# Prompt logits as two products over stacked parts, and five gate units between the mixer's projections and its gated linear unit

## The chip, the cores and the metric

The kernel runs on one core of one Trainium2 chip. The metric is the device time of one execution in microseconds (us), median over runs. Some work of the core goes on side by side: TensorE (PE, matrix products; PEld is its weight load), VectorE (DVE), ScalarE (ACT), GpSimd (POOL), and the DMA queues, most of which are issued by SyncE (SP). Each engine works through its own instructions in a fixed order and waits where an operand or a buffer isn't ready.

## What is computed

One decoder layer for 1024 prompt tokens and 64 sample tokens (8 sequences of 8), model width 1024. The change touches the token mixer between two feed-forward halves:

```python
q, k, v, xs, ga, gb = split(u @ w_in)                 # 512, 512, 512, 512, 1024, 1024 columns
z = q·k * 64**-0.5 + bias                             # 8 heads of 64; key before query only
log_beta = log_sigmoid(z)
log_keep = where(mask, log_beta - z, 0)
after = reverse_cumsum(log_keep) - log_keep
a = where(mask, exp(log_beta + after), 0) @ v         # stick-breaking attention
b = GLU(gelu(S5_scan(xs)))                            # diagonal state-space scan, 32 groups
h = h + g2 * ((sigmoid(ga) * (a @ w_branch_a) + sigmoid(gb) * (b @ w_branch_b)) @ w_out)
```

## The kernel before

Every float32 matrix is held as two float16 parts, hi and lo, and a product is three products: hi·hi, hi·lo, lo·hi. All 1088 token columns (with padding 1092) go through TensorE as three chunks of 364.

The mixer has this order in the code. First the projection of `xs` (the scan's input), then k, then q, each as units of 128 output rows (`project`, L226: 3 chunks of 24 matmuls, so 72 per unit), then v with tokens on the partitions (L1344: 18 chunks of 24 matmuls). The scan `ssm_run` runs for four groups m = 0 to 3, and its steps are issued between these units (list `steps`). Each group sends its result to HBM in eight transfers (`yd`, L995) and loads its matrices in eight and one (`m`, L976 and `ca`, L978) before its last block of matmuls (L988, L990). Then comes the gated linear unit `glu`: its input is split into parts on ACT and DVE (tile `z2`), its products are L226 with operand `z2`, and its output `ob` goes to HBM (`od`, L1444).

Then comes the prompt attention, by pairs of heads (p = 0 to 3), each with 12 steps of 128 keys against the queries not before them: two runs of 128, 256, 384 and 512 queries, and four more of 512. A step computes the logits of two heads (L1087), `ae` and `az` from them (L1094 on ACT, L1095 on DVE), exp, ln and parts (`weights_of`, L1012 to L1028, over both heads at once), sums over keys by triangular products (L1024, L1100), and the product with v (L1105). The sample tokens' attention is issued between. L1056 on ACT, in `scaled_pair`, writes the hi part of q and k back in place, once per pair and operand.

The 16 units of `ga` and `gb` (gate units) have no reader until the branches. One is issued in `glu`, 15 with the attention, paced by a count of its steps. Each evicts three chunks on ACT (L1357) and stores them to HBM (`gd`); the branches read them back. After the attention, `o2` is split and branch b's first products (L216) run.

The code gives the work its dependences and a preference; a scheduler in the compiler puts each engine's instructions in one static order, by its own estimate of times.

The logits of a pair before are three products per head, each over 64 partitions:

Of the kernel before, what the change touches and what calls it, by code (L numbers as in the profile page):

```python
# [9 lines left out]
F32 = mybir.dt.float32  # L10
F16 = mybir.dt.float16
# [9 lines left out]
P = 128  # L21
# [5 lines left out]
NP = 1024  # L27
# [78 lines left out]
class Weights:  # L106
# [88 lines left out]
    def next(self):  # L195
        self.ahead()
        return self.ready.pop(0)
# [835 lines left out]

def halves_of(t, p):

    return t.bitcast(F16).rearrange("p a (t two) -> p a two t", two=2)[:, p, :, :NP]


def scaled_pair(k, qT, kT, p):


    nc = k.nc
    v = nc.vector
    scratch = k.small.tile([P, 16], F32, tag="sq", bufs=1)
    m, r, sc, b = (scratch[:, i:j] for i, j in ((0, 2), (2, 4), (4, 8), (8, 9)))
    for i, t in enumerate((qT, kT)):
        absmax(k, t[:, p, :NP], m[:, i:i + 1])
    nc.gpsimd.partition_all_reduce(r, m, P, ABSMAX)
    v.tensor_single_scalar(sc[:, 2:4].bitcast(I32), r.bitcast(I32), 0x7F800000, op=ALU.bitwise_and)
    v.tensor_scalar(sc[:, 2:4], sc[:, 2:4], 2.0 ** -20, 2.0 ** -14, op0=ALU.max, op1=ALU.mult)  # L1050
    v.reciprocal(sc[:, 0:2], sc[:, 2:4])
    for i, t in enumerate((qT, kT)):
        hi, lo = (halves_of(t, p)[:, j] for j in range(2))
        h = k.part_slot()
        split(k, h, lo, t[:, p, :NP], sc[:, i:i + 1])
        nc.scalar.activation(hi, h, AF.Copy)  # L1056
    cs = k.cs_qk[:, p]
    v.tensor_mul(cs[:, 0:1], sc[:, 2:3], sc[:, 3:4])
    v.tensor_mul(b, r[:, 0:1], r[:, 1:2])
    v.scalar_tensor_tensor(b, b, float(DH), k.bias_m, op0=ALU.mult, op1=ALU.add)  # L1060
    s, inv = pow2_scale(k, b)
    v.tensor_single_scalar(cs[:, 1:2], s, 1.0, op=ALU.min)
    v.tensor_scalar(cs[:, 2:3], inv, 1.0, -1.0, op0=ALU.max, op1=ALU.mult)
    return cs[:, 0:1], (cs[:, 1:2], cs[:, 2:3])


def attend_prompt(k, qT, kT, vt, pairs, scales):

    nc = k.nc
    for p in pairs:  # L1070
        (qh, ql), (kh, kl) = ([halves_of(t, p)[:, j] for j in range(2)] for t in (qT, kT))
        inv, c = scales[p]
        for qc in range(2):
# [3 lines left out]
            for j in range(top, -1, -1):  # L1077
# [4 lines left out]
                def logits(az, ae):  # L1082
                    pz = [k.psz.tile([P, 512], F32, tag="z") for _ in range(2)]
                    for i, (a, b) in enumerate(((kh, qh), (kh, ql), (kl, qh))):
                        for h, ps in enumerate(pz):
                            r = slice(64 * h, 64 * h + 64)
                            nc.tensor.matmul(ps[:, :n], a[r, P * j:P * j + P], b[r, cols], start=i == 0, stop=True,  # L1087
                                             skip_group_check=True)
                    for h, ps in enumerate(pz):
                        b = k.bias[:, 2 * p + h:2 * p + h + 1]  # L1090
                        if j >= 4 * qc:
                            nc.tensor.matmul(ps[:, :P], k.ident16, k.causal, start=False, stop=True,
                                             skip_group_check=True)
                        nc.scalar.activation(ae[:, h, :n], ps[:, :n], AF.Abs, scale=inv, bias=b)  # L1094
                        nc.vector.tensor_scalar(az[:, h, :n], ps[:, :n], inv, b, op0=ALU.mult, op1=ALU.add)  # L1095

# [10 lines left out]
                if (qc, j) == (1, 3) and p < 3:  # L1107
                    scales.append(scaled_pair(k, qT, kT, p + 1))
                if j:
# [165 lines left out]
def mixer_a(k, dr, out, u, ivu, par, ds, gd, od):  # L1275
# [50 lines left out]
    def run(n, sink):  # L1326
        for g in range(n):
            for q in range(2):
                project(g, q, sink)
                for m in steps.pop(0) if steps else ():  # L1330
                    next(ssm[m])

    run(2, keep(kT))
    nc.sync.dma_start(out["kT"].rearrange("m p t -> p m t"), kT)
    run(2, keep(qT, DH ** -0.5))
    for g in range(2):
        w = k.w.next()
# [15 lines left out]

    def to_gate(m, iv):
        def f(c, ps):
            t = k.gate_slot()
            nc.scalar.activation(t, ps, AF.Copy, scale=iv)  # L1357
            (nc.gpsimd if m == 15 else nc.sync).dma_start(gd[m, :, c * CH:(c + 1) * CH], t)
        return f

    gates = [lambda g=g, q=q: project(g, q, to_gate, g == 7) for g in range(8) for q in range(2)]
    k.gate_slot = lambda: k.ring.tile([P, T], F32, tag="r", name="gate")[:, :CH]

    def between():
        gates.pop(0)()

    k.cs_qk = k.co.tile([P, 4, 3], F32, tag="csqk")
    k.part_slot = lambda: k.ring.tile([P, NP], F16, tag="hs", bufs=1)
    scales = [scaled_pair(k, qT, kT, 0)]
    ivb = glu(k, dr, ds, od, between)  # L1370
# [137 lines left out]
def trunk_kernel(ctx, tc, dr, out):  # L1508
# [12 lines left out]
    f2 = ffn_order(dr["ffn2_w_in"], [dr["ffn2_w_out_" + c] for c in "abc"])  # L1521
    order = f1 + [(dr["w_in"][i], KD, 256) for i in (6, 7, 2, 3, 0, 1, 4, 5)]
    order += [(dr["glu_w"][i], 4, 256) for i in range(2)]
    order += [(dr["w_in"][i], KD, 256) for i in range(8, 16)]
    order += [(dr["w_branch_" + n][g], 4, 512) for n in "ba" for g in range(2)]
# [293 lines left out]
```

## Time and profile before

| what | value |
|---|---|
| median of 3 runs (lowest, highest) | 2405.1 us (2403.59, 2409.14) |
| profiled execution, its time | 2406.67 us |
| its span, first to last instruction | 2405.0 us |
| mean granted TensorE clock, of full | 0.982 |

The span is a single execution's; some 1.7 us of its time lie around it. The profiled execution is 1.6 us above the median, so a sum made in its span is moved to the median as a difference.

### The profile page before, as it was taken

How to read it: one execution, taken by the hardware profiler on the slowest of the kernel's cores; microseconds unless marked ns; L12 is line 12 of the kernel's file. 1: busy time of each engine (PE TensorE's matmuls, PEld its weight loads, DVE VectorE, ACT ScalarE, POOL GpSimd, SP SyncE). 2: the span in 40 equal slices, each digit the busy share in tenths (PEclk: the TensorE clock that was granted, in tenths of full speed). 3: DMA queues.
4: the chain of work that ended last, by engine and by line, in shares of the span. 5: the costliest groups of instructions: out<-in, count | busy, mean ns of one | idle time of the engine just before them, and what ended most of it. 6: DMA issues, size and time to landing. Idle time of an engine off the chain costs nothing.

```text
span 2405.0 us, 43066 instructions
## 1 busy us (share of the span) xinstructions
PE 2322.1 (97%) x18535; PEld 1630.6 (68%) x18535; DVE 1689.3 (70%) x3042; ACT 953.8 (40%) x1193; POOL 143.1 (6%) x193
## 2 busy tenths in 40 slices
PE   5999999999999999999999998999999999999997
PEld 2677778777787566775444444656688878888884
DVE  4776688876897726457889887597487654777735
ACT  3443331233331522155778776324343331333403
POOL 0000000000000000001233200000000000000000
PEclk8999999999999999799999999999999999999999
DMA  8133334433343144444233314522101133111302
GB/s 309 53 110 110 110 112 137 151 127 123 119 154 111 66 145 136 113 138 153 73 110 107 106 37 174 173 80 86 61 36 53 52 127 120 64 54 54 128 19 75
DMA packets 90351, 256.54 MB, mean 107 GB/s; under 512 B 12384, under 2 KB 49632, under 8 KB 79920
## 3 DMA queue, kind: packets, MB, share of 16 engines
q1 hardware_dynamic: 84400, 236.16, 28.4%
q0 software_dynamic: 5312, 17.34, 2.4%
q8 instruction: 145, 2.38, 0.4%
q14 instruction: 46, 0.38, 0.1%
q10 hardware_dynamic: 448, 0.29, 0.0%
HBM read 204.10 MB, written 49.66 MB: 106 GB/s over the span
## 4 chain that ended last, share of the span: by engine, by line
PE 44%; DVE 6%; ACT 3%; DMA 2%; issue 1%; POOL 0%; DVEq 0%; POOLq 0%; ACTq 0%
PE u L477 14%; PE u L242 10%; PE u L226 9%; PE u L216 3%; PE z L1087 2%; PE o L1105 1%; PE P L1024 1%; PE P L1100 1%; DVE wl L102 1%; DVE mx L89 1%; PE z L1148 1%; DMA wf<-in_w_in 1%; ACT x L392 0%; DVE mh L102 0%; DMA wf<-in_ffn_w_out_a 0%
## 5 line engine op out<-in xcount | busy, mean ns | idle before, releaser
L226 PE MATMUL u<-u,wh 128*128 128x364 f16 (+1 forms) x1632 | 393.0, 319 | 9.5 <-ACT u L394 6.3
L242 PE MATMUL u<-h,wh 128*128 128x272 f16 (+1 forms) x2304 | 365.9, 280 | 6.1 <-DVE h L102 6.0
L101 ACT ACTIVATE wh<-wf,sc 128x1024 f16<-128x1024 f32 (+2 forms) x128 | 182.3, 1427 | 377.1 <-PE u L242 145.0
L242 PEld LDWEIGHTS <-wh 128*128 128x128 f16 x2816 | 273.1, 97 | 67.1 <-issue 10.4
L89 DVE TENSOR_REDUCE mx<-wf 128x1 f32<-128x1024 f32 (+2 forms) x134 | 210.9, 1597 | 138.7 <-DMA wf<-in_ffn_w_in 77.6
L477 PE MATMUL u<-u,wh 128*128 128x272 f16 x1728 | 272.9, 279 | 0.3 <-DVE q L499 0.3
L477 PEld LDWEIGHTS <-wh 128*128 128x128 f16 x2304 | 221.7, 98 | 63.6 <-issue 19.6
L226 PE MATMUL u<-u,wl 128*128 128x364 f16 (+1 forms) x816 | 260.2, 319 | 1.1 <-DVE wl L102 1.1
L226 PEld LDWEIGHTS <-wh 128*128 128x128 f16 x1824 | 176.6, 98 | 122.2 <-issue 26.0
L102 DVE SCALAR_TENSOR_TENSOR wl<-wf,sc,wh 128x1024 f16<-128x1024 f32 (+2 forms) x128 | 208.7, 1631 | 64.2 <-ACT wh L101 63.4
L242 PE MATMUL u<-h,wl 128*128 128x274 f16 (+1 forms) x1152 | 227.6, 279 | 0.0
L477 PEld LDWEIGHTS <-w3h 128*128 128x128 f16 x1728 | 167.1, 97 | 38.9 <-issue 4.5
L477 PE MATMUL u<-fac,w3h 128*128 128x272 f16 (+1 forms) x1152 | 182.5, 279 | 0.0
L477 PE MATMUL u<-u,wl 128*128 128x272 f16 x864 | 170.3, 278 | 0.0
L82 POOL PARTITION_ALL_REDUCE am<-mx x106 | 54.7, 521 | 1906.9 <-DVE mx L89 1827.7
L242 PEld LDWEIGHTS <-wl 128*128 128x128 f16 x1408 | 136.6, 97 | 29.4
L226 PEld LDWEIGHTS <-wl 128*128 128x128 f16 x912 | 89.4, 98 | 69.0 <-issue 17.9
L477 PEld LDWEIGHTS <-wl 128*128 128x128 f16 x1152 | 111.9, 97 | 24.7 <-issue 0.4
L226 PEld LDWEIGHTS <-aside 128*128 128x128 f16 x864 | 83.0, 97 | 50.5 <-issue 1.7
L477 PE MATMUL u<-fac,w3l 128*128 128x272 f16 x576 | 113.8, 279 | 0.0
L503 ACT ACTIVATE h<-h,iv 128x546 f32<-128x546 f32 x36 | 27.0, 749 | 206.2 <-DVE h L502 206.2
L477 PE MATMUL u<-fac,wh 128*128 128x272 f16 x576 | 92.8, 284 | 3.8 <-DVE st L519 3.8
(430 smaller groups left out, 3922.8 us busy)
## 6 DMA issues: line engine op xcount, KB each, us to landing
wf<-in_ffn_w_in SPq DMA_DIRECT2D x44, 1024.0 KB, 4.8
aw<-in_ada_w SPq DMA_DIRECT2D x72, 512.0 KB, 4.7
wf<-in_w_in SPq DMA_DIRECT2D x16, 1024.0 KB, 5.1
wf<-in_ffn_w_out_a SPq DMA_DIRECT2D x16, 640.0 KB, 3.9
xd<-xr SPq DMA_DIRECT2D x16, 546.0 KB, 2.8
x<-xd SPq DMA_DIRECT2D x16, 546.0 KB, 7.1
xd<-x SPq DMA_DIRECT2D x6, 1456.0 KB, 6.5
sg<-gd SPq DMA_DIRECT2D x16, 546.0 KB, 4.2
```

Source lines behind the costliest of these rows:

```text
L82: k.nc.gpsimd.partition_all_reduce(r, m, P, ABSMAX)
L89: k.nc.vector.tensor_reduce(m, src, axis=axis, op=ALU.max, apply_absolute_value=True)
L101: r = k.nc.scalar.activation(hi, src, AF.Copy, scale=s)
L102: k.nc.vector.scalar_tensor_tensor(lo, src, s, hi, op0=ALU.mult, op1=ALU.subtract)
L216: k.nc.tensor.matmul(ps[:, c, :n], wt[:, cols], act(kt, part)[:, c * CH:c * CH + n], start=kt == 0 and j == 0, stop=kt == nk - 1 and j == 2)
L226: k.nc.tensor.matmul(ps[:, :n], wt[:, cols], act(kt, part)[:, c * CH:c * CH + n], start=kt == 0 and j == 0, stop=kt == nk - 1 and j == 2)
L242: k.nc.tensor.matmul(ps[:, a:b], wt[:, cols], act(kt, part)[:, a0 + a:a0 + b], start=kt == 0 and j == 0, stop=kt == nk - 1 and j == 2)
L477: nc.tensor.matmul(t[:, c0:c1], wt[:, kt * P:kt * P + P], act(kt, part)[:, c0 - 240:c1 - 240], start=first and kt == 0 and j == 0, stop=kt ...
L503: nc.scalar.activation(h2, h2, AF.Silu, scale=iv)
L1024: nc.tensor.matmul(acc[:rk, h, :], k.tri[:rk, :rk], part[:, h, :], start=first and j == 0, stop=True, skip_group_check=True)
L1087: nc.tensor.matmul(ps[:, :n], a[r, P * j:P * j + P], b[r, cols], start=i == 0, stop=True, skip_group_check=True)
L1100: nc.tensor.matmul(acc[:, h, q0:], k.earlier, part[:, h, :], start=False, stop=True, skip_group_check=True)
```

## The change

Two things change. The parts of q and k are stacked on partitions, so that a head's logits are two products over 128 partitions: kh stands on 64 of them and kl on the other 64, against qh on both halves in the first product and ql on both in the second (kl·ql, which was left out before, comes along). The stacking is done by 12 transfers per pair inside SBUF (L1058, 64 rows by 1024 columns of float16 each, 128 KB), from slots that `ah` of the attention uses too. `az` of the second head of each pair is computed on ACT (L1096) and no longer on DVE. The copies L1056 are gone.

Of the gate units, two are issued between q and v, two between v and `glu`, one in `glu` and 11 with the attention. Their slot in the mixer is a ring of two chunks of its own (`gs`), and their weights stand earlier in the list of loads.

```diff
-def halves_of(t, p):
-
-    return t.bitcast(F16).rearrange("p a (t two) -> p a two t", two=2)[:, p, :, :NP]
...
+    qs = pool.tile([P, 2, 2, NP], F16, tag="qs", bufs=1)
+    ks = kT[:, p, :NP].bitcast(F16).rearrange("p (h n) -> p h n", h=2)
     for i, t in enumerate((qT, kT)):
-        hi, lo = (halves_of(t, p)[:, j] for j in range(2))
-        h = k.part_slot()
-        split(k, h, lo, t[:, p, :NP], sc[:, i:i + 1])
-        nc.scalar.activation(hi, h, AF.Copy)
+        parts = [k.part_slot() for _ in range(2)]
+        split(k, *parts, t[:, p, :NP], sc[:, i:i + 1])
+        for h in range(2):
+            own = slice(64 * h, 64 * h + 64)
+            other = slice(64 - 64 * h, 128 - 64 * h)
+            for j, part in enumerate(parts):
+                for rows in (own, other) if i == 0 else ((own, other)[j],):
+                    nc.sync.dma_start(qs[rows, h, j] if i == 0 else ks[rows, h], part[own])
...
                     pz = [k.psz.tile([P, 512], F32, tag="z") for _ in range(2)]
-                    for i, (a, b) in enumerate(((kh, qh), (kh, ql), (kl, qh))):
+                    for i in range(2):
                         for h, ps in enumerate(pz):
-                            r = slice(64 * h, 64 * h + 64)
-                            nc.tensor.matmul(ps[:, :n], a[r, P * j:P * j + P], b[r, cols], start=i == 0, stop=True,
-                                             skip_group_check=True)
+                            nc.tensor.matmul(ps[:, :n], ks[:, h, P * j:P * j + P], qs[:, h, i, cols], start=i == 0,
+                                             stop=True, skip_group_check=True)
...
-                        nc.vector.tensor_scalar(az[:, h, :n], ps[:, :n], inv, b, op0=ALU.mult, op1=ALU.add)
+                        if h:
+                            nc.scalar.activation(az[:, h, :n], ps[:, :n], AF.Identity, scale=inv, bias=b)
+                        else:
+                            nc.vector.tensor_scalar(az[:, h, :n], ps[:, :n], inv, b, op0=ALU.mult, op1=ALU.add)
...
     run(2, keep(kT))
     nc.sync.dma_start(out["kT"].rearrange("m p t -> p m t"), kT)
     run(2, keep(qT, DH ** -0.5))
+    for _ in range(2):
+        between()
+        for m in steps.pop(0) if steps else ():
+            next(ssm[m])
...
-    scales = [scaled_pair(k, qT, kT, 0)]
+    scales = [scaled_pair(k, qT, kT, 0, k.qkv)]
+    for _ in range(2):
+        between()
     ivb = glu(k, dr, ds, od, between)
...
-    order = f1 + [(dr["w_in"][i], KD, 256) for i in (6, 7, 2, 3, 0, 1, 4, 5)]
+    order = f1 + [(dr["w_in"][i], KD, 256) for i in (6, 7, 2, 3, 0, 1, 8, 4, 5, 9)]
     order += [(dr["glu_w"][i], 4, 256) for i in range(2)]
-    order += [(dr["w_in"][i], KD, 256) for i in range(8, 16)]
+    order += [(dr["w_in"][i], KD, 256) for i in range(10, 16)]
```

The change moves instructions at three places. The first is SP's queue behind the scan's third group, before:

```order
L995 DMA yd<-y 16x8x136 x8
L122 DMA wf<-in_glu_w 128x1024
L995 DMA yd<-y 16x8x136 x8
L976 DMA m_10984<-gp 16x8x128 x8
L978 DMA ca<-ca 128x1152
L1351 DMA out_fin<-fin 128x32
L1352 DMA out_fins<-fins 128x256
L1416 DMA y<-yd 128x1088
```

and now (the last group's operands are `m_10984` and `ca`; `qs` and `kT` are the stacked parts):

```order
L995 DMA yd<-y 16x8x136 x8
L122 DMA wf<-in_w_in 128x2048
L995 DMA yd<-y 16x8x136 x8
L976 DMA m_10984<-gp 16x8x128 x8
L978 DMA ca<-ca 128x1152
L1340 DMA gd<-gate 128x364 x2
L1371 DMA out_fin<-fin 128x32
L1372 DMA out_fins<-fins 128x256
L1340 DMA gd<-gate 128x364 x4
L1058 DMA qs<-hs 64x1024
L122 DMA wf<-in_glu_w 128x1024
L995 DMA yd<-y 16x8x136 x8
```

The last group's operands still stand right behind the third group's eight stores; gate stores and the stacking of the first pair follow. On PE, the matmuls of v between the third group's last block and the fourth's go from 96 (four chunks) to 48 (two). Ahead of the third group's first products (L942) 108 matmuls of units stand where 55 did, and ahead of the fourth's 67 where none did.

The second place is PE's queue now, at the last matmuls of a gate unit (L226 with `u`) in the attention:

```order
L226 LDWEIGHTS wl
L226 MATMUL u<-u,wl 128x360
L1103 LDWEIGHTS earlier
L1103 MATMUL P<-ah,earlier 128x512
L1103 LDWEIGHTS earlier
L1103 MATMUL P<-ae,earlier 128x512
```

No gate matmul follows. Of the attention's 96 groups of logits (one per head and step) 70 stand ahead of this place and 26 behind it. Before the change gate matmuls stood among the groups up to the last one, and 56 behind the last product with v.

The third place is the end of ACT's queue in the attention, before (L1357 evicts gate chunks):

```order
L1013 ACTIVATE ae<-ae 128x1024
L1357 ACTIVATE gate<-u,iv 128x364 x2
L1017 ACTIVATE ah<-ae,csqk 128x1024
L1028 ACTIVATE az<-az 128x1024
L1357 ACTIVATE gate<-u,iv 128x364
L1028 ACTIVATE az<-az 128x1024
L1112 ACTIVATE qT<-o 128x512
L1357 ACTIVATE gate<-u,iv 128x364 x2
```

and now:

```order
L1094 ACTIVATE ae<-z,bias,csqk 128x512 x2
L1017 ACTIVATE ah<-ae,csqk 128x1024
L1096 ACTIVATE az<-z,bias,csqk 128x512
L1028 ACTIVATE az<-az 128x1024
L1012 ACTIVATE ae<-ae 128x1024
L1013 ACTIVATE ae<-ae 128x1024
L1017 ACTIVATE ah<-ae,csqk 128x1024
L1028 ACTIVATE az<-az 128x1024 x2
L1115 ACTIVATE qT<-o 128x512
```

A step of 512 queries now has seven ACT instructions (L1094 twice, L1096, L1012, L1013, L1017, L1028) where it had six, and none of gate units stands among them here.

## Rows read from the trace of the kernel before

**Rows 1.** Page, part 1: busy time of each engine, its share of the span, instructions.
```profile
PE 2322.1 (97%) x18535; PEld 1630.6 (68%) x18535; DVE 1689.3 (70%) x3042; ACT 953.8 (40%) x1193; POOL 143.1 (6%) x193
```

**Rows 2.** Windows by stage: length, PE, PEld, DVE, ACT, POOL busy, PEclk, DMA share, GB/s.
```profile
967.00:1060.90 93.90, 88.30 (x641) 73.75 (x641) 43.31 (x104) 26.85 (x42) 1.07 (x3) 0.85 0.43 125
...
1112.80:1475.90 363.10, 361.03 (x2446) 170.67 (x2446) 320.77 (x431) 280.15 (x392) 79.63 (x72) 1.00 0.28 89
```

**Rows 3.** Windows: 20 us of gate units; 20 us of the scan.
```profile
860.00:880.00 20.00, 20.00 (x132) 12.63 (x130) 7.73 (x11) 5.12 (x7) 1.20 (x1) 1.00 0.67 200
980.00:1000.00 20.00, 16.58 (x77) 13.03 (x77) 11.49 (x38) 2.06 (x6) 0.00 (x0) 0.60 0.45 138
```

**Rows 4.** Timeline, PE, the scan: start, us, engine, line, tiles, [idle before <-releaser].
```profile
969.90 2.61 PE L942 MATMUL z<-u,m 128*64 128x136 f32 x24 [2.18 <-ACT y L992]
...
985.21 3.89 PE L942 MATMUL z<-u,m 128*64 128x136 f32 x32 [3.42 <-DMA m<-m]
...
1004.66 0.60 PE L1344 MATMUL z<-wh,u 128*128 128x256 f16 x2
...
1016.71 1.09 PE L988 MATMUL z<-u,m 128*128 128x136 f32 x8
```

**Rows 5.** Timeline, SP queue, the issues behind the third scan block.
```profile
1005.08 3.64 SPq L995 DMA_DIRECT2D yd<-y  x8
1008.81 3.70 SPq L976 DMA_DIRECT2D m<-gp  x8
1012.61 0.38 SPq L978 DMA_DIRECT2D ca<-ca  x1
```

**Rows 6.** DMA issues, 900 to 1120: xcount, KB each, median us to landing.
```profile
ca<-ca SPq DMA_DIRECT2D x4, 576.0 KB, 4.3
```

**Rows 7.** Timeline, PE, groups of prompt logits and their neighbours.
```profile
1099.28 0.35 PE L1087 MATMUL z<-qT,kT 64*128 64x128 f16 x6
1099.57 0.28 PE L1092 MATMUL z<-causal,ident 128*128 128x128 bf16 x2
...
1112.75 0.50 PE L1087 MATMUL z<-qT,kT 64*128 64x256 f16 x3 [1.84 <-DVE az L1095]
...
1327.70 0.33 PE L226 MATMUL u<-u,wh 128*128 128x364 f16 x1
1327.96 0.34 PE L1087 MATMUL z<-qT,kT 64*128 64x128 f16 x3
1328.23 0.23 PE L1092 MATMUL z<-causal,ident 128*128 128x128 bf16 x1
...
1336.00 0.85 PE L1087 MATMUL z<-qT,kT 64*128 64x512 f16 x3
1336.77 0.23 PE L1092 MATMUL z<-causal,ident 128*128 128x128 bf16 x1
```

**Rows 8.** Timeline, ACT, steps of 512 queries, back to back.
```profile
1435.46 0.77 ACT L1094 ACTIVATE ae<-z,bias,csqk 128x512 f32<-128x512 f32 x1
1436.12 1.05 ACT L1013 ACTIVATE ae<-ae 128x1024 f32<-128x1024 f32 x1
1437.07 0.78 ACT L1094 ACTIVATE ae<-z,bias,csqk 128x512 f32<-128x512 f32 x1
...
1439.80 1.15 ACT L1017 ACTIVATE ah<-ae,csqk 128x1024 f16<-128x1024 f32 x1
1440.85 1.04 ACT L1013 ACTIVATE ae<-ae 128x1024 f32<-128x1024 f32 x1
```

**Rows 9.** Groups by line and form, 1114 to 1490: busy us, mean ns, idle before.
```profile
L1357 ACT ACTIVATE gate<-u,iv 128x364 f32<-128x364 f32 x43 | 23.8, 556 | 15.2 <-PE u L226 15.1
```

**Rows 10.** Timeline, PE, the end of the attention.
```profile
1475.78 0.33 PE L226 MATMUL u<-u,wh 128*128 128x364 f16 x1
...
1484.39 1.09 PE L216 MATMUL u<-ob,wh 128*128 128x364 f16 x6
...
1501.88 0.46 PE L216 MATMUL u<-ob,wh 128*128 128x364 f16 x1 [6.21 <-DVE mt L1486]
```

More of the change, by code (lines that the diff above doesn't have):

```diff
@@ L1031, in weights_of, with scaled_pair @@
     return w
-def halves_of(t, p):
-    return t.bitcast(F16).rearrange("p a (t two) -> p a two t", two=2)[:, p, :, :NP]
-def scaled_pair(k, qT, kT, p):
+def scaled_pair(k, qT, kT, p, pool):
     nc = k.nc
@@ L1063, in scaled_pair @@
     v.tensor_scalar(cs[:, 2:3], inv, 1.0, -1.0, op0=ALU.max, op1=ALU.mult)
-    return cs[:, 0:1], (cs[:, 1:2], cs[:, 2:3])
+    return qs, ks, cs[:, 0:1], (cs[:, 1:2], cs[:, 2:3])
 def attend_prompt(k, qT, kT, vt, pairs, scales):
@@ L1070, in attend_prompt @@
     for p in pairs:
-        (qh, ql), (kh, kl) = ([halves_of(t, p)[:, j] for j in range(2)] for t in (qT, kT))
-        inv, c = scales[p]
+        qs, ks, inv, c = scales[p]
         for qc in range(2):
@@ L1107, in attend_prompt @@
                 if (qc, j) == (1, 3) and p < 3:
-                    scales.append(scaled_pair(k, qT, kT, p + 1))
+                    scales.append(scaled_pair(k, qT, kT, p + 1, (k.qkv, k.ring)[(p + 1) % 2]))
                 if j:
@@ L1331, in run, with to_gate, f, between @@
                     next(ssm[m])
+    def to_gate(m, iv):
+        def f(c, ps):
+            t = k.gate_slot()
+            nc.scalar.activation(t, ps, AF.Copy, scale=iv)
+            (nc.gpsimd if m == 15 else nc.sync).dma_start(gd[m, :, c * CH:(c + 1) * CH], t)
+        return f
+    gates = [lambda g=g, q=q: project(g, q, to_gate, g == 7) for g in range(8) for q in range(2)]
+    k.gate_slot = lambda: k.ring.tile([P, CH], F32, tag="gs", bufs=2, name="gate")
+    def between():
+        gates.pop(0)()
     run(2, keep(kT))
@@ L1352, in mixer_a @@
     nc.sync.dma_start(out["fins"], k.fins)
[L1354 to L1365, printed above, removed]
     k.cs_qk = k.co.tile([P, 4, 3], F32, tag="csqk")
-    k.part_slot = lambda: k.ring.tile([P, NP], F16, tag="hs", bufs=1)
-    scales = [scaled_pair(k, qT, kT, 0)]
+    k.part_slot = lambda: k.ring.tile([P, NP], F16, tag="r", name="hs")
+    scales = [scaled_pair(k, qT, kT, 0, k.qkv)]
+    for _ in range(2):
+        between()
     ivb = glu(k, dr, ds, od, between)
```

## The prediction

> **What bounds the kernel now.** I read the page first. TensorE is busy in 97% of the span and no other engine in more than 70% [rows 1], so the sum goes by PE's queue: what it no longer has to do, what it no longer waits for, and where another engine begins to set its pace. Then I read windows by stage. In the prompt attention, PE is busy 361.03 of 363.10 us at full clock, DVE 320.77 and ACT 280.15 [rows 2]: PE binds, and the other two are close enough to take over if PE gets cheaper. In the stretch from the end of q to the first logits' place in the old order (967.0 to 1060.9, with v in it) PE is busy 88.30 of 93.90 us, but its granted clock is 0.85 on average [rows 2], and 0.60 in the 20 us around the scan's last groups [rows 3]. The timeline shows why: PE idles 2.18 us for a scan output's eviction and 3.42 us for a transfer [rows 4]; after that idle the granted clock stays at the lower of its two levels (1.2 instead of 2.4 GHz) for a while. This stretch has waste that other matmuls could fill; the attention has nearly none.
>
> **Part 1: four gate units between q and glu.** A window that holds only unit matmuls has 132 in 20 us [rows 3], so a unit of 72 costs 10.9 us, and four cost 43.6. They lie in PE's queue where the waste was: 108 and 67 of their matmuls ahead of the third and fourth group's first products. That covers both idles (93.90 − 88.30 = 5.6 us) and keeps the clock up. At 0.85 the lost clock is 0.15 × 88.3 = 13.2 us; some of that stretch is overhead that doesn't halve, so of 18.8 I count 18 as given back.
>
> A wait appears as well. The fourth group's last block (L988) needs `m` and `ca`, which SP issues behind the eight stores of the third group: stores from 1005.08, loads from 1008.81, `ca` at 1012.61 [rows 5], landing 4.3 us later [rows 6], so at some 1016.9. The third group's block ends at 1004.66, and L988 runs at 1016.71 without idle [rows 4], because four chunks of v, half of them at the low clock, fill those 12 us. Now only two chunks stand there: 48 matmuls of 256 columns, 5.1 us at 2.4 GHz. SP's order at this place is the same, so PE waits 12.1 − 5.1 = 7 us less what SP gains, 6.3, and then runs slowly for a while (2 us lost). This part is **+43.6 − 18 + 8.3 = +34 us** on this stretch. Its ends: +27 if the fourth group's loads come in time, +43 if the waits merely move. ACT's evictions (L1357, 0.556 us each [rows 9]) and gate stores are covered by a chunk's 3.6 us on PE.
>
> `glu` keeps its waits: its input's hi part stands in ACT's queue behind the evictions of what precedes it, before and now. Nothing is counted there.
>
> **Part 2: logits.** Before, the three 512-column products of a head take 0.77 us to the next matmul (1336.00 to 1336.77), which is 1536 columns at 2.4 GHz plus 0.13; entering the half-height tile from full-height work costs about 0.1 more (1327.70 to 1327.96 for a matmul of 364 columns, 0.15) [rows 7]. So a 512 group costs some 0.88, a 128 group (0.27 + 0.11) 0.38 [rows 7], and by the same 3n/2.4 GHz + 0.24 the others 0.72 and 0.56. The new group is two full-height products, 0.43, 0.32, 0.21, 0.11. The saving is 0.45, 0.40, 0.35 and 0.27 us; with 48 groups of 512 and 16 of each other width, 21.6 + 16.3 = 38 us at most. If entering and leaving costs the same as before, only the columns count: one third of 96 groups' stream, 36,864 columns, **15.4 us at least**. I take 33: the entry is in the rows wherever full-height work precedes, but a part of it stays where L1105, with its half-width tile, is the neighbour.
>
> The Trainium skill says the contrary of the first end: in "TensorE: Matmul & The Clock Gate", section "Part 3: Packing small matmuls — row/col tiling", matmuls on distinct row groups run concurrently. By that, the two heads' products would have shared the array, and the change would add a stream instead of removing two. The trace disagrees: in the one step where the heads alternate, six products of 128 columns take 0.29 us to the next matmul [rows 7], near the 0.32 of six in a row and not the 0.16 of three; elsewhere the order has three of one head in a row.
>
> **Part 3: the stacking and ACT.** Twelve transfers per pair cost SP's queue about 0.46 us each by the eight loads' 3.70 [rows 5], and 2 to 5 us to land ([rows 6] for a larger one). For the first pair two gate units (22 us) follow v and cover it; for the others, issued in the third step from a pair's end, three steps. I count nothing, 4 us for each pair if uncovered. ACT loses the copies L1056 (six in the stage) and four units' evictions, and gains `az` of one head, which DVE loses. Starts 1435.46 and 1436.12 give 0.66 us for a 512 wide one, starts 1436.12 to 1437.07 0.95 and 1439.80 to 1440.85 1.05 for those over both heads [rows 8]. A 512 step takes ACT 2 × 0.66 + 3 × 0.95 + 1.05 = 5.2 us before and 5.9 now; 24 such steps and the narrow ones add some 27 us to ACT; twelve fewer evictions (0.556 us each [rows 9]), the copies and half of the splits take over half of that away again, and ACT stays under PE while there are units.
>
> **Part 4: the attention's end.** Because all units are issued by the 70th of 96 groups, the last pair's 12 steps have no filler. There a 512 step costs PE sixteen streams of 512 columns, 3.4 to 3.6 us, while ACT needs 5.9: ACT sets the pace. Six such steps are 35.4 us; the six narrow ones (1.5 × 512 columns per run of three, plus fixed parts) I take at 19. With 5 for waits between engines and 5 to drain, the last pair lasts 65 us, where PE has 31.5 to do.
>
> From 1099.3, where the unit in `glu` ends and the first logits stand [rows 7], to 1475.8, behind the last product [rows 10], PE spent 376.5 us, 1.84 of them idle ahead of the second step [rows 7]. It had 155 us of units there (15 × 10.9 less the 8.6 that stand behind, 1475.78 to 1484.39 [rows 10]); now 11 units, 120. So 374.7 − 155 + 120 − 33 = 306.7, of which 31.5 in the last pair: 275 us to its start, +65, +3 for the wait at the start: **343 instead of 376.5, −33.5 us** (−50 if the tail loses half as much, −21.5 if it takes 77).
>
> At the very end, the 8.6 us of units behind the last product are gone, and L216 follows at once [rows 10]; the 6.21 us wait behind it remains, since `o2` and the gate products start earlier by as much: **−8.6**, at least −5.
>
> **Sum.** +34 − 33.5 − 8.6 = −8.1 us. The profiled execution's span of 2405.0 (its time is 2406.67) becomes some 2397 (2398.6); its time lies 1.6 above the median of the runs, so on that median of 2405.1 the same difference gives **2397 us**. A measurement of this kernel tells 0.2% (4.8 us) from no change, so that is a gain, by a little.
>
> **Rivals.**
> *A, the tail is slower (not faster):* without filler each step waits in turn for PE, ACT, DVE and back; in the old trace PE's work between hid this. If a 512 step takes 7.1 instead of 5.9 for the last 26 groups, ten such steps and narrow ones cost +15: 2412. It decides from about 73 us for the last pair. For it: DVE is also at 88% in the stage. Against it: ACT's rows at the end stand back to back [rows 8], two steps interleaved. In the Trainium skill, "TensorEngine Tiling (Array Packing)", section "PSUM Bottleneck", says that a faster TensorE doesn't speed up PSUM evacuation, which may become the bottleneck; that would be this case.
> *B, the waste moves (no change):* the fourth group's wait is longer or the clock falls again, and part 1 costs +43: 2406.
> *C, the tail overlaps well (faster):* the scheduler has run ahead on ACT and DVE, so the tail loses only half of its 33.5 us: −17 more, 2380.
> *D, the logits save only columns:* 15.4 instead of 33, in the part that PE binds: +17, 2414.
> *E, the two heads did run at once:* the array's stream grows by one 512 per step (0.21, 0.16, 0.11, 0.05 us for 24, 8, 8, 8 steps, 7.7 us) instead of −33: 2438.
>
> **Chances.** Forecast 0.43, A 0.17, B 0.15, C 0.18, D 0.05, E 0.02. Of the forecast (2388 to 2403) 0.38 and all of C are faster by over 0.2%: 0.56. The rest of the forecast (0.05), most of B (0.12) and the mild end of A (0.05) are within 0.2%: 0.22. The rest of A (0.12) and B (0.03), D and E are slower: 0.22. The range from 2380 (C) to 2414 (A, D) leaves out the far ends. The forecast's own range is 2388 to 2403.
>
> **What would show it.** Right: the clock near 1.0 from q to glu, with one idle gap of some 6 us before L988 of the fourth group; L1087 with 192 matmuls of 128 rows, busy 30 to 40 us in place of 65; in the last 65 us of the attention ACT at 95% and PE near 50%; L216 directly after the last product with v. Wrong: gaps in the tail with ACT idle too (A); waits on the stacked parts (`qs`, `kT`) before the first logits of a pair; the low clock in the tail, where slow matmuls would lengthen each step's chain; or a wait in `glu` grown by the stacking's transfers ahead of its loads.

## The result

The changed kernel takes 2431.4 us (median of 4 runs, 2430.38 to 2434.75) against 2404.35 us for the kernel before (median of 4). The ratio is 1.0112, with a 95% interval of 1.0093 to 1.0131: slower by 27 us, where 8 us faster was forecast. The profiled execution took 2430.38 us with a span of 2428.7, 23.7 us more than the span of 2405.0 before.

The page of the changed kernel, span and part 1 [rows 1]:

```profile
span 2428.7 us, 42932 instructions
...
PE 2300.0 (95%) x18439; PEld 1631.1 (67%) x18439; DVE 1663.9 (69%) x2994; ACT 966.2 (40%) x1233; POOL 142.3 (6%) x193
```

PE has 22 us less to do, and the kernel is slower. The windows by stage tell where (columns as in [rows 2]): up to glu's first product, from there to the last pair of heads, the last pair, and 20 us of the scan [rows 3].

```profile
967.00:1106.40 139.40, 122.60 (x922) 93.85 (x920) 58.08 (x123) 38.66 (x60) 2.10 (x6) 0.93 0.48 147
1106.40:1422.80 316.40, 306.20 (x2183) 163.64 (x2182) 255.47 (x335) 250.28 (x362) 83.76 (x78) 0.98 0.39 121
1422.80:1506.40 83.60, 54.97 (x228) 20.28 (x226) 64.15 (x73) 62.93 (x89) 0.00 (x0) 0.80 0.20 76
980.00:1000.00 20.00, 20.00 (x143) 14.00 (x143) 10.46 (x35) 1.77 (x5) 0.00 (x0) 1.00 0.48 160
```

Before, the first stretch was 93.9 us long, and now it is 139.4, with four more units in it. In those 20 us of the scan PE no longer idles, at full clock instead of 0.60. In the last pair PE is busy 54.97 of 83.6 us. PE's timeline at the places that decide (start, us, tiles, idle before and its releaser):

```profile
1014.85 2.15 PE L988 MATMUL z<-u,m 128*128 128x136 f32 x8 [4.68 <-DMA m<-gp]
...
1094.01 0.39 PE L1087 MATMUL z<-qs,kT 128*128 128x128 f16 x4
...
1106.39 1.07 PE L226 MATMUL u<-z,wh 128*128 128x364 f16 x3 [11.88 <-ACT z L101]
...
1399.53 0.59 PE L1087 MATMUL z<-qs,kT 128*128 128x512 f16 x2
1399.96 0.32 PE L226 MATMUL u<-u,wl 128*128 128x364 f16 x1
...
1422.81 0.29 PE L1087 MATMUL z<-qs,kT 128*128 128x128 f16 x2
...
1451.30 1.12 PE L1108 MATMUL o<-az,vt 128*64 128x512 f32 x2 [2.46 <-ACT az L1028]
...
1506.37 1.09 PE L216 MATMUL u<-ob,wh 128*128 128x364 f16 x3
...
1523.15 1.98 PE L216 MATMUL u<-ob,wh 128*128 128x364 f16 x6 [4.96 <-DVE mt L1495]
```

The fourth scan group's block waits 4.68 us [rows 4]. Glu's first product waits 11.88 us. A head's 512 wide logits take 0.43 us (1399.53 to 1399.96), where they took 0.77 to the next matmul [rows 7]. The last pair starts at 1422.81, and the products with v wait for ACT there. L216 follows the last product at 1506.37, and the branches go on at 1523.15 [rows 10].

The difference by stages, from starts of matmuls: glu's first product came at 1060.90 and comes at 1106.39, +45.5. From there to the end of the last product it was 414.9 us and is 400.0, −14.9. From there to the branches' restart (1501.88 and 1523.15) it was 26.1 and is 16.8, −9.3. That is +21.3; another 2.4 come behind it, which no run here takes apart (in the 10 us from the restart the granted clock is 0.75 now and 0.78 before).

The wait ahead of glu, as the timeline of all engines shows it:

```profile
1073.79 0.16 DVE L89 TENSOR_REDUCE mx<-zm 128x1 f32<-128x4 f32 x1
...
1094.06 1.15 ACT L101 ACTIVATE wh<-wf,sc 128x1024 f16<-128x1024 f32 x1 [2.90 <-PE u L226]
...
1095.24 1.28 DVE L102 SCALAR_TENSOR_TENSOR wl<-wf,sc,wh 128x1024 f16<-128x1024 f32 x1 [8.22 <-ACT wh L101]
...
1096.55 0.33 SPq L122 DMA_DIRECT2D wf<-in_w_in  x1
...
1101.39 2.29 DVE L89 TENSOR_REDUCE mx<-wf 128x1 f32<-128x2048 f32 x1 [4.86 <-DMA wf<-in_w_in]
...
1103.84 0.68 POOL L82 PARTITION_ALL_REDUCE am<-mx  x2 [17.40 <-DVE mx L89]
...
1104.56 0.15 DVE L74 TENSOR_SCALAR sz<-am 128x1 int32<-128x1 int32 x1 [0.17 <-POOL am L82]
...
1105.13 2.30 ACT L101 ACTIVATE z<-zg,sz 128x1092 f16<-128x1092 f32 x2 [9.48 <-DVE sz L76]
```

The last unit ends at 1094, and only then ACT writes the next weight's hi part (L101, released by PE's L226: the buffer was in use). DVE's lo part follows (L102), and frees the buffer of the load; SP issues that load at 1096.55; DVE's maximum of the loaded weight (L89) runs at 1101.39. Glu's own scale (`sz`, L74) stands behind that maximum in DVE's order, though the last of the maxima that it needs (`mx` from `zm`, first row) was taken 30 us earlier. GpSimd's order has it so too: its reductions over partitions (`am`, L82) run one behind the other at 1103.84, the weight's and then glu's, after 17.40 us of idle. The split of glu's input starts at 1105.13, and PE gets it at 1106.39.

### The profile page after: what moved, and what is told of

It is laid out like the page before. It is cut to its first block, busy times and chain, and to the rows that moved or that the text cites. A ratio compares the mean times of both kernels' runs of the same rounds, so it can differ in the third digit from the quotient of the medians.

```text
span 2428.7 us, 42932 instructions
## 1 busy us (share of the span) xinstructions
PE 2300.0 (95%) x18439; PEld 1631.1 (67%) x18439; DVE 1663.9 (69%) x2994; ACT 966.2 (40%) x1233; POOL 142.3 (6%) x193
## 4 chain that ended last, share of the span: by engine, by line
PE 59%; DVE 11%; ACT 5%; DMA 4%; issue 3%; POOL 1%; SPq 1%; DVEq 0%; POOLq 0%; ACTq 0%
PE u L477 20%; PE u L242 14%; PE u L226 13%; PE u L216 3%; PE z L1364 2%; DVE wl L102 1%; DVE mx L89 1%; DMA wf<-in_w_in 1%; PE P L1024 1%; PE z L990 1%; PE o L1108 1%; PE z L226 1%; ACT ae L1094 1%; PE z L1151 1%; DMA aw<-in_ada_w 1%
## 5 line engine op out<-in xcount | busy, mean ns | idle before, releaser
L226 PE MATMUL u<-u,wh 128*128 128x364 f16 (+1 forms) x1632 | 388.4, 319 | 9.6 <-ACT u L394 6.3
L101 ACT ACTIVATE wh<-wf,sc 128x1024 f16<-128x1024 f32 (+2 forms) x128 | 182.4, 1427 | 377.0 <-PE u L242 168.9
L89 DVE TENSOR_REDUCE mx<-wf 128x1 f32<-128x1024 f32 (+2 forms) x134 | 211.0, 1597 | 153.0 <-DMA wf<-in_ffn_w_in 78.0
L102 DVE SCALAR_TENSOR_TENSOR wl<-wf,sc,wh 128x1024 f16<-128x1024 f32 (+2 forms) x128 | 208.8, 1631 | 97.7 <-ACT wh L101 97.2
L226 PEld LDWEIGHTS <-wh 128*128 128x128 f16 x1824 | 176.9, 98 | 130.4 <-issue 28.9
L226 PE MATMUL u<-u,wl 128*128 128x364 f16 (+1 forms) x816 | 259.9, 319 | 1.1 <-DVE wl L102 1.1
L82 POOL PARTITION_ALL_REDUCE am<-mx x106 | 55.7, 532 | 1924.8 <-DVE mx L89 1845.5
L226 PEld LDWEIGHTS <-wl 128*128 128x128 f16 x912 | 89.3, 98 | 61.0 <-issue 6.9
L226 PEld LDWEIGHTS <-aside 128*128 128x128 f16 x864 | 83.0, 97 | 50.5 <-issue 1.7
```

Source lines behind the costliest of these rows:

```text
L82: k.nc.gpsimd.partition_all_reduce(r, m, P, ABSMAX)
L89: k.nc.vector.tensor_reduce(m, src, axis=axis, op=ALU.max, apply_absolute_value=True)
L101: r = k.nc.scalar.activation(hi, src, AF.Copy, scale=s)
L102: k.nc.vector.scalar_tensor_tensor(lo, src, s, hi, op0=ALU.mult, op1=ALU.subtract)
L226: k.nc.tensor.matmul(ps[:, :n], wt[:, cols], act(kt, part)[:, c * CH:c * CH + n], start=kt == 0 and j == 0, stop=kt == nk - 1 and j == 2)
```

## Experiments

Each ratio is to the kernel before, with runs on the same chip. Chips differ (the kernel before took 2402 to 2418 us on them), so ratios are compared, and times within a profile.

| kernel | ratio, 95% interval |
|---|---|
| logits_alone | 0.9989, 0.9969 to 1.0009 |
| units_alone | 1.0210, 1.0186 to 1.0234 |
| stores_on_act | 1.0141, 1.0115 to 1.0166 |
| units_after_split | 1.0031, 1.0020 to 1.0043 |
| logits_late_stack | 0.9947, 0.9925 to 0.9969 |
| logits_az_dve | 1.0020, 1.0002 to 1.0039 |
| tail_filled | 1.0056, 1.0037 to 1.0074 |
| two_late_stack | 1.0009, 0.9995 to 1.0024 |
| all_early | 1.0553, 1.0529 to 1.0578 |
| late_paced | 1.0454, 1.0433 to 1.0475 |
| two_paced | 1.0433, 1.0416 to 1.0450 |
| five_paced | 1.0445, 1.0423 to 1.0466 |
| tail_hot | 1.0019, 1.0000 to 1.0039 |
| split_again | 1.0034, 1.0016 to 1.0052 |
| before_late | 0.9993, 0.9979 to 1.0007 |
| late_again | 0.9927, 0.9906 to 0.9949 |

**Each part alone.** logits_alone takes out the early units:

```diff
-    for _ in range(2):
-        between()
-        for m in steps.pop(0) if steps else ():
-            next(ssm[m])
...
-    for _ in range(2):
-        between()
     ivb = glu(k, dr, ds, od, between)
...
-... (6, 7, 2, 3, 0, 1, 8, 4, 5, 9)]
+... (6, 7, 2, 3, 0, 1, 4, 5)]
```

> The stacked logits with az of one head on ACT, and the gate units where they were before (one in glu, 15 with the attention). Theory T (the loss of the change comes from the moved units: 11.9 us of idle PE ahead of glu's products, and a last pair of 83.6 us because no unit is left to fill it): the wait in glu is that of before (some 3.4 us), units last to the attention's end, and PE saves some 27 us of logits time: 2377 to 2390. Rival R (the new logits form itself makes the attention slow: ACT does a seventh instruction per step, and the parts come by transfers): not faster than before, 2400 or more.

units_alone is the kernel before with that same code put in:

> The five early units as in the change, the logits as before (three products, az on DVE). Theory T: the wait of some 12 us ahead of glu's products is there too, the scan's waste (18 us less a new wait of 8) is given back, and the attention's end has no units, so its last pair costs 70 us or more where PE has 41 to do: 2415 to 2440. Rival R (the units are harmless, the new logits cost the time): 2390 to 2405.

The units alone cost 2.1%, more than the whole change. Theory T was right on the units in kind, but the loss is larger than the 2415 to 2440 us that it allowed. It was wrong on the logits: they alone gained nothing measurable. The two parts don't add up: without the early units the new logits give 0.1%, with them 1.0% (1.0210 and 1.0112). Two waits in PE's timeline of logits_alone show part of it:

```profile
1063.20 0.58 PE L1087 MATMUL z<-qs,kT 128*128 128x128 f16 x4 [5.37 <-ACT vt L1362]
...
1070.55 0.77 PE L226 MATMUL u<-z,wh 128*128 128x364 f16 x2 [6.55 <-ACT z L101]
```

The first pair's logits, which now stand ahead of glu in PE's order, wait 5.37 us, and glu's input comes 6.55 us later still: glu's first product starts at 1070.55 instead of 1060.90. Rival R named two causes; the next experiments take them one by one.

**The wait ahead of glu.** stores_on_act and units_after_split:

```diff
-            (nc.gpsimd if m == 15 else nc.sync).dma_start(gd[m, ...], t)
+            (nc.gpsimd if m == 15 else nc.scalar if m < 4 else nc.sync).dma_start(gd[m, ...], t)
```

> The change, with the gate stores of the first four units issued from ACT's queue, each right behind its eviction, so that SP is free for the next weight's load. Theory T1 (the wait ahead of glu is SP's: the load of the next gate weight stands behind gate stores that wait for evictions): the idle of 11.9 us falls to 4 or less, 2414 to 2421. Theory T2 (the load waits for its buffer, which is freed only when the units' matmuls are done and ACT and DVE have split the weight before it, and DVE's order has that weight's maximum ahead of glu's scale): the idle stays at 10 to 12 us, 2426 to 2434.

```diff
-    for _ in range(2):
-        between()
     ivb = glu(k, dr, ds, od, between)
...
         split(k, z2[m][:, 0, :], z2[m][:, 1, :], zg[m], s)
+    for _ in range(2):
+        between()
     for g in range(2):
```

> The change, with the two units ahead of glu issued in the code behind the split of glu's input instead of ahead of it; PE's order at this place stays (two units, then glu's products), but DVE's order has glu's scale and split right behind the maxima of its input, ahead of the next weight's maximum. Theory T2: the idle of 11.9 us ahead of glu's products is gone (under 2 us), with the low clock behind it: 13 to 16 us less than the change, 2415 to 2419. Theory T1 (SP's gate stores) or a chain that starts in glu's input itself: the idle stays, 2427 to 2434.

With the stores on ACT's queue, glu's first product still waits 11.79 us:

```profile
1111.03 0.39 PE L1087 MATMUL z<-qs,kT 128*128 128x128 f16 x4
...
1123.32 1.07 PE L226 MATMUL u<-z,wh 128*128 128x364 f16 x3 [11.79 <-ACT z L101]
```

With the units behind the split in the code, it follows the last unit's matmul without idle (first row: the unit; second: glu):

```profile
1096.70 0.32 PE L226 MATMUL u<-u,wl 128*128 128x360 f16 x1
1096.85 0.47 PE L226 MATMUL u<-z,wh 128*128 128x364 f16 x2
```

So SP's queue wasn't the cause (T1 fell; at 1.0141 its interval touches the change's, so whether the ACT-issued stores cost anything isn't shown). The place of the units in the code was, as T2 said: now glu's reduction and scale stand ahead of the next weight's maximum on GpSimd and DVE alike, and which of the two orders alone would have held glu up was not tried. The ratio went from 1.0112 to 1.0031, some 19 us, more than the wait and the clock behind it; the static order behind it differs too.

**The first pair's stacking.** logits_late_stack is logits_alone with it issued inside glu:

```diff
-    scales = [scaled_pair(k, qT, kT, 0, k.qkv)]
-    ivb = glu(k, dr, ds, od, between)
+    scales = []
+    ivb = glu(k, dr, ds, od, between, lambda: scales.append(scaled_pair(k, qT, kT, 0, k.qkv)))
...
         split(k, z2[m][:, 0, :], z2[m][:, 1, :], zg[m], s)
+    stack()
     for g in range(2):
```

> As logits_alone, with the splitting and stacking of the first pair issued behind the split of glu's input instead of ahead of glu. Theory S (in logits_alone glu's products started 9.6 us later than before because the first pair's split and its twelve transfers stand ahead of glu's loads and its work on ACT and DVE): glu's products start as before, 8 to 11 us less than logits_alone, some 0.994 to 0.996 of before. Rival (the delay has another cause, or the first logits now wait for their parts instead): like logits_alone, 0.998 to 1.001 of before.

It is faster than the kernel before, 0.9947. The two waits are gone: glu's first product waits 0.92 us and starts at 1053.95. A start by itself says little, though: in late_again, the same program, it comes at 1062.98 with the same wait of 0.92, since the scan took 9 us longer there (144.4 us from its first product to glu's, and 135.2). before_late puts the same edit into the kernel before, without the new logits, and late_again repeats logits_late_stack beside it:

> The kernel before, with one thing changed: the first pair's scaling and splitting is issued behind the split of glu's input, as in logits_late_stack. If the gain of logits_late_stack (0.9947) is that of the logits, this is 0.998 to 1.001 of before. If most of it came from glu's earlier start (1053.9 against 1060.9), this is 0.995 to 0.998, and the new logits are worth under 0.3% by themselves, since the attention's chain doesn't get shorter.

> logits_late_stack once more, beside before_late on the same chip: 0.993 to 0.997 of before.

before_late gains nothing (0.9993). In its trace glu starts at 1054.88, and from there to the last product with v it takes 424.3 us instead of 414.9. So the gain comes with the new logits and not with the later splitting: 0.7% by the two ratios (16 us), 13 us by the medians. It includes what `az` on ACT and the change's gate ring give, which stand in late_again too.

**az on DVE.** logits_az_dve is logits_alone with L1096 taken out and both heads' az on DVE:

> As logits_alone, with az of both heads on DVE as before the change. Theory A (PE saves some 25 us of logits in the attention but gives 20 back in short waits, since ACT has a seventh instruction per step): PE's waits in the attention fall by half or more, 8 to 12 us less than logits_alone, 0.994 to 0.996 of before. Rival D (DVE, 88% busy in the attention before, then sets the pace): no gain, 0.998 to 1.005 of before, with PE's waits put down to DVE.

It is 1.0020 where logits_alone had 0.9989; theory A fell. ACT's seventh instruction does no harm that shows. That moving `az` off DVE is worth 0.3% is likely but not shown: the two intervals just touch.

**What bounds the last pair.** tail_filled, and with `3 * (hi, lo)` tail_hot, are units_after_split with this in `rest`:

```diff
+                    if p == 3 and j < top:
+                        for h in range(2):
+                            for part in (hi, lo):
+                                nc.tensor.matmul(po[64 * h:64 * h + 64, q0:], k.none, part[:, h, :], start=False,
+                                                 stop=False, skip_group_check=True)
```

> As units_after_split, with four more matmuls per step in the last pair of heads: the parts against a stationary operand of zeros, added to the output's accumulation (they add zero), so PE has more to do there and its order is else the same. Theory C (the last pair takes 83.8 us because PE falls to the low clock there, and slow matmuls stand in every step's chain): the granted clock stays up and the last pair takes 65 to 76 us, up to 0.7% less than units_after_split. Rival P (ACT, DVE and the waits between them set the pace whatever the clock): 82 us or more, not faster than units_after_split.

> As tail_filled (which added four matmuls per step of the last pair that add zero, and left its 83.8 us and a granted clock of 0.83), with twelve per step. Theory C (the low clock makes the last pair long): the granted clock rises to 0.95 or more and the last pair takes 76 us or less. Theory P (the chain over PE, ACT and DVE sets its pace): 82 to 88 us at whatever clock.

> units_after_split once more, beside tail_hot on the same chip: 1.001 to 1.005 of before, the last pair 82 to 86 us. Theory P has tail_hot at the same time within 0.2% or up to 0.3% above, theory C has it 0.3% or more below.

The windows of the last pair, of tail_hot and then of its base:

```profile
1417.70:1500.90 83.20, 65.12 (x324) 26.39 (x322) 64.14 (x73) 63.73 (x90) 0.00 (x0) 0.85 0.21 80
```

```profile
1418.50:1501.90 83.40, 56.52 (x227) 20.46 (x224) 63.86 (x73) 63.70 (x90) 0.00 (x0) 0.79 0.21 79
```

In tail_filled too it took 83.9 us. PE did 8.6 us more in tail_hot and the pair took as long (83.2 and 83.4), and the two kernels' intervals overlap. The clock rose only to 0.85, so this run doesn't reach the clock that theory C asked for. logits_alone does: there units stand in the last pair, the clock is 0.98, and up to its last product it takes the same time with twice the matmuls:

```profile
1394.80:1478.00 83.20, 76.96 (x447) 38.03 (x445) 68.80 (x80) 69.03 (x102) 1.62 (x2) 0.98 0.15 51
```

So between 227 and 447 matmuls, and between clocks of 0.79 and 0.98, the last pair's length in these kernels moves by less than 1 us. The two went up together, so a gain by the clock that the added matmuls took up again isn't excluded.

The trace of the change shows where much of the time goes. It is in the two places where the steps run out, in the middle of the pair and at its end:

```profile
1435.32 0.38 PE L1087 MATMUL z<-qs,kT 128*128 128x512 f16 x1 [0.52 <-DVE az L1098]
...
1439.38 0.63 PE L1225 MATMUL z<-ident,os 128*128 128x128 f32 x4 [0.21 <-DVE az L1098]
...
1441.80 0.66 PE L1225 MATMUL z<-ident,os 128*128 128x128 f32 x4 [0.35 <-ACT az L1096]
...
1453.95 0.69 DVE L89 TENSOR_REDUCE mo<-qT 128x1 f32<-128x512 f32 x1 [3.79 <-ACT qT L1115]
1454.67 1.20 DVE L1229 TENSOR_TENSOR qT<-qT,z 64x128 f32<-64x128 f32 x4
1455.31 0.40 PE L1087 MATMUL z<-qs,kT 128*128 128x128 f16 x2 [2.04 <-DVE qT L1229]
...
1484.89 0.59 PE L1087 MATMUL z<-qs,kT 128*128 128x512 f16 x2
```

The fourth step's logits start at 1435.3, the fifth's at 1455.3: 20 us (19 to 22 in every kernel here but the paced ones, where they are longer). TensorE writes logits into two buffers (`z`), one for each head of a step. At 1439.38 and 1441.80 the sample tokens' transposes (L1225) take both, and what empties these (L1229) stands in DVE's order behind a maximum (L89) over the first run's output, which is there only after that run's last product with v. The last step's logits start at 1484.9, and its products with v end at 1506.4: 21.5 us more. Windows of 10 us (columns as in [rows 2]: two around the start of the break, two from the second run) show that ACT is nearly full while the steps follow each other, and idle for more than half of the break:

```profile
1432.80:1442.80 10.00, 6.92 (x45) 3.33 (x43) 8.16 (x11) 9.97 (x17) 0.00 (x0) 1.00 0.00 0
1442.80:1452.80 10.00, 4.61 (x18) 1.16 (x15) 6.05 (x5) 4.03 (x4) 0.00 (x0) 0.83 0.00 0
1462.80:1472.80 10.00, 8.30 (x32) 3.37 (x31) 7.97 (x10) 9.71 (x15) 0.00 (x0) 0.64 0.00 0
1472.80:1482.80 10.00, 7.45 (x21) 2.04 (x21) 8.66 (x8) 9.70 (x12) 0.00 (x0) 0.70 0.00 0
```

No run moved L1229 or gave `z` a third buffer, so what that would give isn't known.

**The attention without units.** all_early:

```diff
         split(k, z2[m][:, 0, :], z2[m][:, 1, :], zg[m], s)
+    for _ in range(12):
+        between()
+    stack()
     for g in range(2):
...
-... (6, 7, 2, 3, 0, 1, 8, 4, 5, 9)]
+... (6, 7, 2, 3, 0, 1, 8, 4, 5, 9, 10, 11, 12, 13, 14)]
```

> The change with 14 of the 16 units ahead of glu's products (behind the split of its input, as in units_after_split), one in glu and one at the attention's start, so that 46 of the attention's 48 steps have no unit at all; the first pair's stacking behind glu's split. It shows what the attention takes without anything to fill it. Theory P (the steps' chain over PE, ACT and DVE sets the pace; the last pair takes 83 to 90 us in every kernel so far, with 228 matmuls in it or with 521): each of the four pairs takes 80 to 95 us, the attention 340 to 370 us, as long as with units in it, and the whole is 60 us or more slower than before, 1.025 to 1.045. Theory W (ACT's work sets the pace, as the prediction had it: 55 to 65 us a pair): 235 to 270 us for the attention, and the whole comes near the time before, 0.985 to 1.005.

Its four pairs, by windows:

```profile
1240.50:1352.50 112.00, 81.79 (x432) 35.25 (x429) 77.76 (x110) 77.67 (x109) 26.84 (x26) 0.71 0.28 85
1352.50:1452.10 99.60, 67.88 (x430) 27.21 (x429) 71.86 (x104) 70.55 (x103) 30.63 (x30) 0.83 0.34 94
1452.10:1544.60 92.50, 61.04 (x399) 24.66 (x398) 62.51 (x76) 64.55 (x96) 15.56 (x16) 0.76 0.24 63
1544.60:1626.80 82.20, 55.41 (x227) 20.59 (x224) 61.51 (x72) 62.62 (x89) 0.00 (x0) 0.79 0.20 77
```

and those of the kernel before, with the old logits and nearly all of the units in them:

```profile
1099.30:1208.20 108.90, 106.43 (x711) 52.37 (x711) 90.54 (x130) 79.74 (x110) 28.50 (x27) 0.98 0.33 113
1208.20:1302.20 94.00, 93.27 (x675) 43.70 (x674) 84.22 (x112) 74.00 (x103) 34.77 (x30) 1.00 0.36 107
1302.20:1386.00 83.80, 83.66 (x630) 39.69 (x629) 74.90 (x109) 66.98 (x96) 19.32 (x19) 1.00 0.30 98
1386.00:1475.80 89.80, 89.23 (x521) 42.14 (x519) 79.06 (x96) 66.78 (x90) 0.71 (x2) 1.00 0.15 48
```

386.3 us with PE busy 266, against 376.5 with PE busy 372.6. Without units, no engine is busy over 77% of a pair's time, and three of the four pairs are longer, not shorter. PE's largest waits there are L1103 for DVE's L1026 (21.4 us), L1024 for DVE's L1021 (14.8) and logits for `az` (16.2 for both engines). Theory P held in kind, with pairs of 82 to 112 us where it said 80 to 95 and a worse time than it said (1.055), and theory W fell. The granted clock is 0.71 to 0.83 here and was 0.98 to 1.00 before; how long the steps would take without units at the full clock no run shows.

**Units spread by hand.** late_paced, two_paced and five_paced cut the units of logits_late_stack, two_late_stack and the mended change into thirds and hold each behind the product with v of a step (the lines that cut them are left out here):

```diff
-        while n_gates - len(gates) < (n_gates - 3) * done / steps:
-            gates.pop(0)()
+        while gates and n_gates - len(gates) < 2 + (n_gates - 2) * done / 46:
+            with tc.issue_after(k.behind.ins):
+                gates.pop(0)()
```

> The change with only the two units between q and v moved (one in glu, 13 with the attention), and the first pair's stacking behind the split of glu's input. If the waits found so far are the causes (units in front of glu's split and the stacking ahead of it; a last pair with nothing to fill it), the scan's waste is given back (some 10 us net), glu starts without a new wait, and the attention saves some 9 us as in logits_alone, less what the shorter supply of units costs at its end: 0.992 to 0.997 of before. If moved units cost by themselves: 1.000 or more.

> As logits_late_stack (units where they were before the change), with the units cut into thirds of 24 matmuls which are held behind the product with v of one step each, so that they stand spread over all 48 steps. Theory P: the attention is bound by PE where units stand thick and by the chain where they stand thin; spread evenly, less of either is lost, 4 to 12 us less than logits_late_stack, 0.990 to 0.994 of before. Rival (blocks of 24 matmuls, 3.6 us, stand in the chain's way as often as they fill it): no gain, 0.994 to 1.000.

> As two_late_stack (two units between q and v, one in glu, 13 with the attention), with the units held and spread in thirds as in late_paced. Theory P: the last ten steps are no longer without units, so the units fill idle PE there and the head gets shorter: 8 to 20 us less than two_late_stack, 0.993 to 0.997 of before. Rival: no gain, 1.000.

> The change with all three mends: the two units ahead of glu and the first pair's stacking behind the split of glu's input, and the 11 units of the attention held and spread in thirds. Theory P: the attention can't get shorter than its chain, some 340 to 360 us, so the early units cost what they no longer fill: 0.998 to 1.003 of before, and not faster than late_paced. Rival W (spread units let the attention shrink by all the work that left it): 0.985 to 0.993.

two_late_stack is as fast as before (1.0009), slower than logits_late_stack: two early units cost some 0.6%. The three paced kernels missed every expectation, by 4%. The four pairs of five_paced:

```profile
1131.90:1271.50 139.60, 102.89 (x603) 50.61 (x601) 87.94 (x120) 83.96 (x117) 28.82 (x29) 0.80 0.34 103
1271.50:1388.80 117.30, 93.66 (x641) 47.04 (x640) 74.24 (x104) 77.31 (x113) 31.84 (x27) 0.88 0.30 90
1388.80:1500.30 111.50, 88.59 (x577) 41.63 (x577) 71.16 (x89) 73.13 (x106) 16.27 (x17) 0.82 0.26 74
1500.30:1600.20 99.90, 74.26 (x383) 35.31 (x381) 65.20 (x76) 68.52 (x96) 2.70 (x4) 0.87 0.24 88
```

PE is busy 359 of 468 us. In its order the units now stand as closed blocks of 24 matmuls (3.6 us each), where the scheduler's own order mostly has one to sixteen between a step's products. That a block in front of a step's products delays the whole step fits that, and was not tried by itself.

## Why the prediction was wrong

**Part 1, the stretch up to glu, was right but for one line.** The clock is 1.00 in the scan and the fourth group's wait came (4.68 us, 6.3 was said). +45.5 less the wait of 11.88 is +33.6, where +34 stood; that it fits to 0.4 us is in part luck, since the scan of one and the same program took 9 us more in late_again than in logits_late_stack. The line that failed is "`glu` keeps its waits ... Nothing is counted there." I looked at ACT's order, where the split stands behind evictions before and after, and not at DVE's and GpSimd's, where a weight's maximum came ahead of glu's scale. These orders were to be had before the run; only what the weight then waits for (its buffer, free when the unit's matmuls end) had to be followed. 12 us, and a few at the low clock.

**Part 2, the logits' price, was right in kind for the order that it met, and misread one step.** Over the starts of all of its matmuls, a 512 group took 0.81 us before (0.88 was said) and 0.45 in the part with units after; over all widths that is some 59 and 32 us, a saving of 27 where 33 stood. Rivals D and E are out as prices. But "The trace disagrees" is wrong. The six products of 128 columns with the heads in turn took 0.35 us from first start to last end, and 0.29 to the next matmul; three of one head in a row took 0.34 and 0.27 [rows 7]. Six in the time of three means that the two heads' products did run side by side. A narrow window shows the first two together, and a 256 wide step with the heads in turn took 0.52 us for six, where three in a row took 0.50 [rows 7]:

```profile
1099.28 0.23 PE L1087 MATMUL z<-qT,kT 64*128 64x128 f16 x2
...
1329.99 0.52 PE L1087 MATMUL z<-qT,kT 64*128 64x256 f16 x6
```

In three of the 48 steps before the heads alternate throughout; elsewhere three products of one head mostly stand together and share nothing. An estimate from these rows: with the heads in turn in every step, a 512 step's old logits would take what one group took, 0.81 us for both heads, less than the 0.90 of the new form, without stacking. No run tried it.

But the sum handed all of the saving to the time. With the units where they were, the new logits and what comes with them are worth 0.7% (13 to 16 us), and only with the first pair's stacking out of glu's way; "I count nothing" for the stacking in part 3 was wrong by 0.4 to 0.6% in logits_alone.

**Part 4 failed in a number and in the idea behind it.** From glu's first product to the last pair's start, the sum says 38.4 (1060.9 to 1099.3) and 278, and 316.4 were measured. That this fits is luck in part: PE was busy 306.2 of them, 7 less than the sum has, and idle 7 more. The last pair then took 83.6 instead of 65: +18.6, and with the 11.9 in glu this is all of the miss of 31.8 us but 1.3. Rival A had this, with 73 us as the point from which it decides, at a chance of 0.17.

The step of the sum that failed is "With 5 for waits between engines and 5 to drain", and not ACT's pace. Over the whole pair ACT and DVE are each busy three quarters of the time, but while the steps follow each other ACT is as full as the prediction said (9.7 of 10 us). A step's work passes from PE to ACT to DVE and back several times: late in the pair a step of 512 takes 21 to 24 us from its logits to its product with v, with three or four steps in flight. So each time the steps run out, the pair waits for most of that: 20.0 us pass at the change of runs, where `z` was held too, and 21.5 behind the start of the last step's logits. The other 42.1 us are the ten intervals between starts within the runs, where 54.4 were counted for twelve steps. Every kernel here but the three paced ones has 82 to 90 us for the last pair, with 228 matmuls or 521.

The first view misled me: PE at 99% busy in the attention, and so I priced each unit taken out at its 10.9 us. all_early shows what those units were: filler in a time that the steps need anyway, at the clock that they then run at. Taken out, they give nothing there, and outside they cost their full price. That is the larger part of units_alone's loss of some 50 us: four units of 43.6 us, a wait of 12 in glu, and little back but 18 us of waste and a shorter end. Its attention even grew, from 414.9 to 429.9 us between glu's first product and the end of the last, which nothing here explains further.

**Part at the end** (−8.6) was right: −9.3.

The range ended at 2414 since A and the wait in glu were never added. What remains open is what mending the break at the change of runs would give, what the clock adds to the steps, and how much of the attention's length the static order makes: from glu's first product to L216 it is 423.5 us in the kernel before and 432.8 in before_late, with the same work in it.

## What to carry to other kernels

A busy engine isn't yet the bound: fillers make it look so. Before pricing work that is moved out of a stretch, ask how long the stretch takes without it; a stretch of the same kernel in which the filler is missing, or an experiment that moves all of it, tells. Count separately the places where a pipeline of steps drains. When work is moved ahead of a stage, follow the order of every engine that feeds the stage's first instruction, and the buffers that the moved work holds. Take a gain in the place where it is real (the new logits alone, with their stacking behind glu's split, run at 0.993 to 0.995 of before) and leave the rest.

## What the runs showed that was not expected

PE was busy 99% of the attention before at full clock, and 69% of the same attention without units, at a mean granted clock of 0.71 to 0.83, for 386 us instead of 376. Twelve extra matmuls per step raised the granted clock of the last pair from 0.79 to 0.85 and left its time as it was. The three kernels with units held by hand took 4.4% more than the kernel before, more than any part of the change cost. And where the two heads' products of half height stood in turn, six took the time of three: 0.52 us against 0.50 at 256 columns.
